# First layer's experts: the loads of the modulation columns issued by GpSimd's queue instead of SyncE's

## The chip, the cores and the metric

The kernel runs on one core of a Trainium2 chip. The metric is the device time of one execution in microseconds (us), as the median of several runs. Engines are named as the profile names them: PE is TensorE (matmuls; PEld is its weight loads, which overlap the matmuls), DVE is VectorE, ACT is ScalarE, POOL is GpSimd, SP is SyncE. A DMA is issued by an engine's instruction queue and then moved by the core's 16 DMA engines. In the profile's table of DMA queues, q1 (hardware) carries what SP issues and q0 (software) what POOL issues.

## The reference, cut to what matters

The reference is a two-layer transformer over 1024 latent tokens and 256 context tokens of width 1024. In each layer a conditioning vector is turned into six modulation vectors, attention and a convolution mix the tokens, and a mixture of 16 experts follows, in which every expert picks its 128 best latent tokens (and, in the first layer alone, its 32 best context tokens):

```python
def adaln(cond, w_mod_l, b_mod_l, n_chunks):
    m = jax.nn.silu(cond) @ w_mod_l[:, :n_chunks * D_MODEL] + b_mod_l[:n_chunks * D_MODEL]
    return jnp.split(m, n_chunks, axis=-1)

def ec_moe(h, w_router, w_gate, w_up, w_down):
    ...
    g, idx = lax.top_k(jnp.swapaxes(aff, 1, 2), cap)
    xs = jax.vmap(lambda hb, ib: hb[ib])(h, idx)
    hid = jax.nn.silu(jnp.einsum('becd,edf->becf', xs, w_gate)) * jnp.einsum('becd,edf->becf', xs, w_up)
    ye = jnp.einsum('becf,efd->becd', hid, w_down) * g[..., None].astype(h.dtype)
    return jax.vmap(lambda yb, ib: jnp.zeros((n_tok, d), h.dtype).at[ib.reshape(-1)].add(yb.reshape(-1, d)))(ye, idx)
```

The modulation of the second layer (`adaln` with that layer's weights) depends on nothing but the conditioning vector. The kernel computes most of it while the first layer's experts run, and the change touches the loads for that.

## The kernel before, in words

**The experts of the first layer.** The loop in `moe` takes 192 steps, numbered i: 16 experts e, each with 12 chunks c of weights of 1 MB (c 0 to 7 are gate and up, c 8 to 11 are down). A chunk lands in a buffer called `raw`, `more` or `srow` (a ring of nine buffers), ACT rounds it to `hi` (line 2078), DVE takes the remainder to `lo` (line 2084), and PE multiplies with both: 12 matmuls per step for the latent tokens (lines 2158 and 2262; of every three, the second is the one with `lo`, and the first of a step's twelve is one with `hi`) and 16 narrow ones for the context tokens straight from the raw chunk (lines 2169 and 2250). In step i, DVE prepares the `lo` of chunk i + 2, and SP issues the load of chunk i + 9, which waits until PE has read the chunk that stands in the same buffer (`w_load`, line 2073).

**POOL** has only DMAs to issue in this stage, four per expert, all with row indices: at c = 2 it gathers the next expert's tokens (`xg` and `xgc`, lines 2111 and 2116), and at the end of c = 11 it adds the expert's result to the sums in DRAM (`s_accc` and `s_acc`, lines 2284 and 2296), after DVE has made `yoc` and `yo`.

**The modulation columns.** In steps with i % 7 == 1 the next of 24 tiles `adw` of 1 MB is loaded (`adaln_load`, line 359), until the list `ad` is empty (i = 1, 8, 15, ... 162). There is one buffer for it. In later steps with i % 7 in 4, 5, 6 or 0 (not where c is 7 or 8), DVE multiplies a half of the tile with the conditioning row and sums it up (`adaln_col`, line 365, written `adj<-adw`): two such instructions in a step, two or four for a tile. Since 7 and 12 have no common divisor, the load falls on every c in turn.

**What sets the order.** The stage runs under `manual_schedule`: each engine and each queue takes its instructions in the order in which this loop writes them, and waits at each until what it needs is there. So DVE's `lo` of a later chunk stands behind the `adj` of the step before.

Of the kernel before, what the change touches and what calls it, by code (L numbers as in the profile page):

```python
# [208 lines left out]
class Kern:  # L209
# [145 lines left out]
        cm.__exit__(None, None, None)  # L355
        self.close(2)

    def adaln_load(self, w, l, t):
        self.nc.sync.dma_start(w, self.d["wmt"][(l * 48 + t - 12) // 2])

    def adaln_col(self, w, junk, l, t, i):

# [1724 lines left out]
    def moe(self, l, out):  # L2087
        nc, d = self.nc, self.d
# [20 lines left out]
        def gather(e):  # L2109
            x = p.tile([128, D], F32, name="xg", bufs=1)  # L2110
            nc.gpsimd.indirect_dma_start(out=x, out_offset=None, in_=self.s_h2,
                                         in_offset=bass.IndirectOffsetOnAxis(ap=idx[:, e:e + 1], axis=0))
            xc = None
            if not last:
                xc = p.tile([32, D], F32, name="xgc", bufs=1)
                nc.gpsimd.indirect_dma_start(out=xc, out_offset=None, in_=self.s_h2c,
                                             in_offset=bass.IndirectOffsetOnAxis(ap=idxc[:32, e:e + 1], axis=0))
            S["x", e] = (x, xc)
# [31 lines left out]
        def mm_gu0(e, c, ns=(0, 2, 1, 3)):  # L2150
            hi, lo = S["w", e, c]
            xt = S["xt", e]
            if c == 0:
                S["gu", e] = [rot(ps, [128, 512], F32, "gu", nb) for _ in range(4)]
            o = S["gu", e]
            for n in ns:
                for i, (a, w) in enumerate(three(hi, lo)):
                    nc.tensor.matmul(o[n], xt[:, c, a], w[:, n], start=c == 0 and i == 0, stop=c == 7 and i == 2)  # L2158
# [20 lines left out]
        def ev_gu0(e, n):  # L2179
            o = S["gu", e]  # L2180
            s = S["s", e, n] = p.tile([128, 512], F32, name="sg", bufs=2)
            nc.scalar.activation(s, o[n], AF.Silu)
            nc.vector.tensor_tensor(s, s, o[2 + n], op=ALU.mult)
# [22 lines left out]
        def mm_gu1(e, c):  # L2206
            hi, lo = S.pop(("w", e, c))
            xt = S["xt", e]
            n, r = divmod(c, 4)
            u, kh = divmod(r, 2)  # L2210
            if kh == 0:
                S["gu", e, n, u] = rot(ps, [128, 512], F32, "gu", 8)
            o = S["gu", e, n, u]
            for k in range(4):
                kk = kh * 4 + k
                nc.tensor.matmul(o, xt[:, kk, 0], hi[:, k], start=kk == 0, stop=False)  # L2216
                nc.tensor.matmul(o, xt[:, kk, 1], hi[:, k], start=False, stop=False)  # L2217
                nc.tensor.matmul(o, xt[:, kk, 0], lo[:, k], start=False, stop=kk == 7)  # L2218

        def ev_gu1(e, c, st):  # L2220
            n, r = divmod(c, 4)
            if st == 0 and r == 1:
                s = p.tile([128, 512], F32, name="sg", bufs=2)
                nc.scalar.activation(s, S.pop(("gu", e, n, 0)), AF.Silu)
                S["s", e, n] = s
            elif st == 0 and r == 3:
                s = S["s", e, n]
                nc.vector.tensor_tensor(s, s, S.pop(("gu", e, n, 1)), op=ALU.mult)
            elif st == 1 and r == 3:
                s = S.pop(("s", e, n))  # L2230
                if n == 0:
                    S["hid", e] = rot(p, [128, KC, 2, 128], F32R, "hid", 1)
                hd = S["hid", e]
                t = rot(ps, [128, 4, 128], F32, "gu", 8)
                for j in range(4):
                    nc.tensor.transpose(t[:, j], s[:, j * 128:(j + 1) * 128], self.ident)  # L2236
                ks = slice(n * 4, n * 4 + 4)
                nc.scalar.activation(hd[:, ks, 0], t, AF.Copy)  # L2238
                nc.vector.tensor_tensor(hd[:, ks, 1], t, hd[:, ks, 0].bitcast(F32), op=ALU.subtract)  # L2239
# [25 lines left out]
        def mm_d1(e, c):  # L2265
            hi, lo = S["w", e, c]
            hd = S["hid", e]
            n, kh = divmod(c - 8, 2)
            if kh == 0:
                S["y", e, n] = rot(ps, [128, 512], F32, "gu", 8)  # L2270
            y = S["y", e, n]
            for k in range(4):
                kk = kh * 4 + k
                nc.tensor.matmul(y, hd[:, kk, 0], hi[:, k], start=kk == 0, stop=False)  # L2274
                nc.tensor.matmul(y, hd[:, kk, 1], hi[:, k], start=False, stop=False)  # L2275
                nc.tensor.matmul(y, hd[:, kk, 0], lo[:, k], start=False, stop=kk == 7)  # L2276
# [11 lines left out]
        def ev_d(e, n):  # L2288
            ns = slice(n * 512, n * 512 + 512)
            y = S["y", e, n]  # L2290
            if n == 0:
                S["yo", e] = rot(p, [128, D], F32, "yo", 1)
            yo = S["yo", e]
            nc.vector.scalar_tensor_tensor(yo[:, ns], y, g[:, e:e + 1], self.g2[0][:, ns], op0=ALU.mult, op1=ALU.mult)  # L2294
            if n == 1:
                nc.gpsimd.indirect_dma_start(out=self.s_acc[l],  # L2296
                                             out_offset=bass.IndirectOffsetOnAxis(ap=idx[:, e:e + 1], axis=0),
                                             in_=yo, in_offset=None, compute_op=ALU.add)
# [30 lines left out]
        ad, todo = [], []  # L2329
        if not last:  # L2330

            ad = [t for j in range(8) for t in (2 * j, 16 + 4 * j, 18 + 4 * j)]
# [8 lines left out]
        for i in range(n - 2 if last else n - 4):  # L2341
            e, c = steps[i] if i < n else (None, None)
            pe, pc = steps[i - 1] if i > 0 else (None, None)
            if c == 2 and e + 1 < NE:
                gather(e + 1)

            def weights():
                if m <= i + m - 1 < n:
                    self.w_hi(i + m - 1)
                if m <= i + m - 2 < n:  # L2350
                    self.w_lo(l, i + m - 2, nc.vector)
            if last:
                if c < 8:
                    mm_gu1(e, c)
                else:
                    mm_d1(e, c)
                if pc is not None and pc < 8:
                    ev_gu1(pe, pc, 0)
                elif pc is not None and pc % 2:
                    ev_d(pe, pc // 2 - 4)  # L2360
                weights()
            elif c < 8:

                if c % 2 == 0:
                    mm_gu0(e, c)
                    mm_gc(e, c)
                else:
                    mm_gc(e, c)
                    if c == 7:
                        ev_gc(e)  # L2370
                    mm_gu0(e, c)
                if c < 7:
                    weights()
                else:
                    ev_gu0(e, 0)
                    ev_gu0(e, 1)
                    hprep(e, 0)
                    if e + 1 < NE:
                        xprep_c(e + 1)
                    hprep_c(e)  # L2380
                    weights()
                    if e + 1 < NE:
                        xprep(e + 1)
            else:
                if c % 2 == 0:
                    mm_d0(e, c)
                    if c == 8:
                        hprep(e, 1)
                    mm_dc(e, c)
                else:  # L2390
                    mm_dc(e, c)
                    mm_d0(e, c)
                weights()
                if c == 11:
                    ev_dc(e)
                    for h in range(2):
                        ev_d(e, h)
            while nl < n and nl - len(self.ring) <= (i + m - 2 if last else i):
                self.w_load(l, nl)
                nl += 1  # L2400
            if last and pc is not None and pc < 8:
                ev_gu1(pe, pc, 1)
            if last and i > n - 12:
                spare(i - n + 11)
            if ad and i % 7 == 1:
                adw = p.tile([128, 2, D], F32, name="adw")
                self.adaln_load(adw, l + 1, ad[0])
                todo = self.adaln_items(l + 1, ad.pop(0))
            elif todo and i % 7 in (4, 5, 6, 0) and c not in (7, 8):
                for f in todo[:2]:  # L2410
                    f(adw, p.tile([128, D], BF16, name="adj"))
                todo = todo[2:]
            if last and c == 9 and e + 1 < NE:
                xprep(e + 1)
# [166 lines left out]
```

## Time and profile before

| | |
|---|---|
| Median of 3 runs | 2855.28 us (2850.66 to 2855.35) |
| Profiled execution | 2855.14 us, of which the profile's span is 2853.4 us |
| Busy in the span: PE, DVE, ACT, POOL | 91%, 73%, 55%, 31% |
| First layer's experts, in the span | about 780 to 1570 us |
| Loads of `adw` in that stage | 24 of 1 MB, issued by SP |

The page gives busy times over the whole span; what the change is worth is read from the stretch of the first layer's experts. "Idle before" in a row is the time in which the engine did nothing ahead of that instruction, with the one that ended the wait behind the arrow. Times at a row's start count from the start of the span.

### The profile page before, as it was taken

Reading aid. Unit: us, or ns where it says so; the run is one execution under the profiler, and the core shown is the slowest. Engines: PE = TensorE matmul, PEld = TensorE weight load, DVE = VectorE, ACT = ScalarE, POOL = GpSimd, SP = SyncE. Lnnn points to the kernel's source line nnn. Section 1 sums busy time; section 2 is a strip of 40 time slices with the busy share of each in tenths; the row PEclk is TensorE's granted clock in tenths of the full one; section 3 lists DMA queues with packets and bytes.
Section 4 is the critical chain, followed back from the end, with each engine's and each line's share of the span. In section 5 each row is a group of like instructions: output and inputs, shape, how many; then the busy total and the mean of one; then the engine's idle time right before and its main releaser. Section 6 shows DMA issues by size and latency. Waiting matters only on the chain. (4 is left out here: it accounts for less than half of the span.)

```text
span 2853.4 us, 34425 instructions
## 1 busy us (share of the span) xinstructions
PE 2585.3 (91%) x12313; PEld 1861.0 (65%) x12313; DVE 2085.5 (73%) x2803; ACT 1559.2 (55%) x1920; POOL 883.7 (31%) x649
## 2 busy tenths in 40 slices
PE   7998999979499999999999599999993899999995
PEld 4986555568466666666666588655573677777774
DVE  6366467768777878787876925566588788888888
ACT  3224678622456555565655434686322577777774
POOL 3046677432410213121130308684132011111113
PEclk8999999989699999999999799999996899999997
DMA  6254644593588988889885415663456699999983
GB/s 252 67 177 156 189 147 124 151 261 119 195 308 304 321 328 307 333 309 343 306 316 196 149 60 181 174 176 93 143 195 250 237 368 373 371 372 374 374 331 139
DMA packets 204342, 682.69 MB, mean 239 GB/s; under 512 B 25637, under 2 KB 97630, under 8 KB 148870
## 3 DMA queue, kind: packets, MB, share of 16 engines
q1 hardware_dynamic: 191834, 641.23, 61.8%
q0 software_dynamic: 12336, 39.25, 5.7%
q8 instruction: 97, 1.59, 0.2%
q14 instruction: 75, 0.61, 0.1%
HBM read 600.45 MB, written 79.84 MB: 238 GB/s over the span
## 5 line engine op out<-in xcount | busy, mean ns | idle before, releaser
L2078 ACT ACTIVATE hi<-raw 128x2048 fp32r<-128x2048 f32 x264 | 505.1, 1916 | 172.0 <-PE gu L2158 78.8
L2084 DVE TENSOR_TENSOR lo<-raw,hi 128x2048 fp32r<-128x2048 f32 x259 | 582.9, 2283 | 13.6 <-ACT hi L2078 13.5
L1258 POOL TENSOR_TENSOR cy<-cy,csq 128x512 f32<-128x512 f32 (+1 forms) x300 | 372.7, 1256 | 111.0 <-ACT csq L1254 102.2
L2158 PE MATMUL gu<-hi,xt 128*128 128x512 f32 x1024 | 343.7, 404 | 0.0
L1184 PE MATMUL O<-P,v 128*65 128x512 f32 (+7 forms) x592 | 275.4, 555 | 7.9 <-ACT P L1177 7.7
L2078 ACT ACTIVATE hi<-more 128x2048 fp32r<-128x2048 f32 x105 | 200.5, 1915 | 139.6 <-PE gu L2158 112.5
L2296 POOL DMA_INDIRECT s_acc<-yo,i x31 | 122.2, 3942 | 492.8 <-DVE yo L2294 488.2
L2084 DVE TENSOR_TENSOR lo<-more,hi 128x2048 fp32r<-128x2048 f32 x105 | 237.2, 2285 | 32.8 <-ACT hi L2078 32.6
L2158 PEld LDWEIGHTS gu<-hi,xt 128*128 128x128 f32 x1024 | 193.5, 189 | 97.8 <-issue 53.6
L1254 ACT ACTIVATE csq<-ch,cw 128x512 f32<-128x512 f32 (+1 forms) x300 | 198.1, 673 | 39.0 <-POOL cy L1258 33.2
L2284 POOL DMA_INDIRECT s_accc<-yoc,i x16 | 23.6, 1474 | 621.6 <-DVE yoc L2283 621.6
L2216 PE MATMUL gu<-hi,xt 128*128 128x512 f32 x512 | 204.1, 399 | 0.0
L2158 PE MATMUL gu<-lo,xt 128*128 128x512 f32 x512 | 203.5, 398 | 0.0
L2217 PE MATMUL gu<-hi,xt 128*128 128x512 f32 x512 | 202.6, 396 | 0.0
L2218 PE MATMUL gu<-lo,xt 128*128 128x512 f32 x512 | 202.3, 395 | 0.0
L735 PE MATMUL pj<-hhi,whi 128*128 128x512 f32 (+1 forms) x512 | 188.4, 368 | 8.8 <-ACT whi L248 8.8
L737 PE MATMUL pj<-hhi,wlo 128*128 128x512 f32 (+1 forms) x512 | 188.0, 367 | 1.1 <-DVE wlo L251 1.0
L736 PE MATMUL pj<-hlo,whi 128*128 128x512 f32 (+1 forms) x512 | 187.6, 366 | 0.0
L2262 PE MATMUL gu<-hi,hid 128*128 128x512 f32 x512 | 173.0, 404 | 0.0
L365 DVE CUSTOM_DVE_ANT_0 adj<-adw,srow,bmod 128x1024 bf16<-128x1024 f32 x96 | 132.9, 1384 | 50.0 <-DMA adw<-in_wmt 48.4
L1177 ACT ACTIVATE P<-ST 128x512 f32<-128x512 f32 (+1 forms) x200 | 114.6, 581 | 55.1 <-PE ST L1160 30.1
L1736 PE MATMUL po<-hi,ohi 128*128 128x512 f32 x288 | 121.9, 423 | 19.3 <-DVE ohi L1714 18.2
(320 smaller groups left out, 5736.1 us busy)
## 6 DMA issues: line engine op xcount, KB each, us to landing
raw<-in_wmoe SPq DMA_DIRECT2D x264, 1024.0 KB
more<-in_wmoe SPq DMA_DIRECT2D x105, 1024.0 KB
adw<-in_wmt SPq DMA_DIRECT2D x24, 1024.0 KB
srow<-in_wmoe SPq DMA_DIRECT2D x15, 1024.0 KB
wraw<-in_win SPq DMA_DIRECT2D x26, 512.0 KB
x<-in_x SPq DMA_DIRECT2D x16, 512.0 KB
adw<-in_wmt SPq DMA_DIRECT2D x16, 512.0 KB
q<-s_q SPq DMA_DIRECT2D x64, 128.0 KB
```

Source lines behind the costliest of these rows:

```text
L735: nc.tensor.matmul(o[:, :w], whi[:, k], hhi[:, k, sl], start=k == 0, stop=False)
L736: nc.tensor.matmul(o[:, :w], whi[:, k], hlo[:, k, sl], start=False, stop=False)
L737: nc.tensor.matmul(o[:, :w], wlo[:, k], hhi[:, k, sl], start=False, stop=k == 7)
L1184: nc.tensor.matmul(o[:V1, o0:o0 + w], self.v[:, t["kt"], t["v"] * V1:t["v"] * V1 + V1], t["P"][:, :w], start=t["first"], stop=t["last"] is ...
L1254: nc.scalar.activation(z[:, :w], h, AF.Copy, scale=c)
L1258: nc.gpsimd.tensor_tensor(st["y"], st["y"], st.pop(("z", t))[:, :w], op=ALU.add)
L2078: self.nc.scalar.activation(h, self.S["raw", i], AF.Copy)
L2084: eng.tensor_tensor(lo, r, h.bitcast(F32), op=ALU.subtract)
L2158: nc.tensor.matmul(o[n], xt[:, c, a], w[:, n], start=c == 0 and i == 0, stop=c == 7 and i == 2)
L2216: nc.tensor.matmul(o, xt[:, kk, 0], hi[:, k], start=kk == 0, stop=False)
L2217: nc.tensor.matmul(o, xt[:, kk, 1], hi[:, k], start=False, stop=False)
L2218: nc.tensor.matmul(o, xt[:, kk, 0], lo[:, k], start=False, stop=kk == 7)
```

## The change

`adaln_load` takes the queue as an argument, and the one call in the experts' loop passes POOL's. The loads in the first layer's start (`adaln_first`) and in the attention stay on SP's queue, as do all loads of expert weights.

```diff
-    def adaln_load(self, w, l, t):
-        self.nc.sync.dma_start(w, self.d["wmt"][(l * 48 + t - 12) // 2])
+    def adaln_load(self, w, l, t, eng=None):
+        (eng or self.nc.sync).dma_start(w, self.d["wmt"][(l * 48 + t - 12) // 2])
...
             if ad and i % 7 == 1:
                 adw = p.tile([128, 2, D], F32, name="adw")
-                self.adaln_load(adw, l + 1, ad[0])
+                self.adaln_load(adw, l + 1, ad[0], nc.gpsimd)
                 todo = self.adaln_items(l + 1, ad.pop(0))
```

PE, DVE and ACT keep their instructions in the same order. On SP's queue the 24 rows go; here around the load of step 71, between the loads of weight chunks:

```order
 L2073 DMA more_8902<-in_wmoe 128x2048
 L2073 DMA more_8937<-in_wmoe 128x2048
-L359 DMA adw<-in_wmt 128x2048
 L2073 DMA raw_8966<-in_wmoe 128x2048
 L2073 DMA raw_8988<-in_wmoe 128x2048
```

The weight loads stand in the order they had, with one load of 1 MB less among them.

On POOL's queue they come in between the DMAs with row indices; here from the end of expert 2 (`s_accc` and `s_acc` with `yoc_7858` and `yo_7863`) to the end of expert 3:

```order
 L2284 DMA s_accc<-yoc_7858,i_6746 512x512
 L2296 DMA s_acc<-yo_7863,i_6721 1024x1024
-L2111 DMA xg<-s_h,i_6721 128x1024
-L2116 DMA xgc<-s_h2c,i_6743 32x1024
+L359 DMA adw<-in_wmt 128x2048
+L2111 DMA xg<-s_h,i_6721 128x1024
+L2116 DMA xgc<-s_h2c,i_6743 32x1024
+L359 DMA adw<-in_wmt 128x2048
 L2284 DMA s_accc<-yoc_8214,i_6746 512x512
 L2296 DMA s_acc<-yo_8219,i_6721 1024x1024
```

The first `adw` (step 36, c = 0) now stands right behind the two additions of expert 2 and ahead of the gathers; the second (step 43, c = 7) stands behind the gathers and ahead of the next additions.

The same at the end of expert 5 (`yo_8933`), where the load of step 71 (c = 11) and that of step 78 (c = 6) come in:

```order
 L2284 DMA s_accc<-yoc_8928,i_6746 512x512
 L2296 DMA s_acc<-yo_8933,i_6721 1024x1024
-L2111 DMA xg<-s_h,i_6721 128x1024
-L2116 DMA xgc<-s_h2c,i_6743 32x1024
+L359 DMA adw<-in_wmt 128x2048
+L2111 DMA xg<-s_h,i_6721 128x1024
+L2116 DMA xgc<-s_h2c,i_6743 32x1024
+L359 DMA adw<-in_wmt 128x2048
 L2284 DMA s_accc<-yoc_9284,i_6746 512x512
```

The load of step 71 stands behind the additions too, and takes the place in POOL's queue that the gather of `xg` had. Of the 24 loads, those of steps 36, 71, 85, 120 and 155 (c = 0, 11, 1, 0, 11) stand so, right behind the additions of an expert; those of steps 15, 50, 99 and 134 (c = 2 or 3) stand right behind the gathers; the other 15 stand where POOL has only the coming additions to wait for.

## Rows read from the trace of the kernel before

**Rows 1.** Busy time in stretches of the first layer's experts: start and end, length, busy time of PE, PEld, DVE, ACT, POOL, granted clock of PE as a share of full speed, share of the DMA engines, GB/s.
```profile
800.00:1080.00 280.00, 279.37 (x1536) 181.78 (x1534) 224.73 (x185) 166.63 (x137) 42.91 (x20) 1.00 0.85 316
1080.00:1430.00 350.00, 346.32 (x1904) 224.76 (x1905) 284.67 (x233) 201.41 (x162) 74.62 (x30) 1.00 0.87 320
```
**Rows 2.** Waits from 780 to 1490 us, of POOL, DVE and PE: who waited for whom, us in total, times, the longest.
```profile
POOL s_accc L2284 <- DVE yoc L2283: 552.0, 14, 49.7
...
DVE adj L365 <- DMA adw<-in_wmt: 14.5, 7, 4.5
...
PE gu L2169 <- DVE yo L2294: 4.3, 2, 2.3
```
**Rows 3.** PE's timeline at the first of its two waits for DVE's `yo`: start, length, instruction.
```profile
1081.38 1.92 PE L2169 MATMUL gu<-raw,xct 128*32 128x512 f32 x16 [2.02 <-DVE yo L2294]
```
**Rows 4.** Two loads of `adw` on SP's queue (steps 36 and 71): start and length of the issue.
```profile
934.32 0.47 SPq L359 DMA_DIRECT2D adw<-in_wmt  x1
...
1077.12 0.33 SPq L359 DMA_DIRECT2D adw<-in_wmt  x1
```
**Rows 5.** POOL's timeline: the addition of expert 2 and the gather of `xg` behind it; the addition of expert 3 and the gather of `xgc` behind it; the addition of expert 5 and the gather behind it; then the gathers behind the additions of experts 6, 9 and 12; the length is the time in which POOL writes the DMA's descriptors.
```profile
933.72 7.32 POOL L2296 DMA_INDIRECT s_acc<-yo,i  x1 [0.30 <-issue]
941.34 1.56 POOL L2111 DMA_INDIRECT xg<-s_h,i  x1 [0.30 <-issue]
...
982.52 1.92 POOL L2296 DMA_INDIRECT s_acc<-yo,i  x1 [0.30 <-issue]
...
987.69 1.78 POOL L2116 DMA_INDIRECT xgc<-s_h2c,i  x1 [0.30 <-issue]
...
1082.73 8.52 POOL L2296 DMA_INDIRECT s_acc<-yo,i  x1 [0.30 <-issue]
1091.55 2.65 POOL L2111 DMA_INDIRECT xg<-s_h,i  x1 [0.30 <-issue]
...
1138.70 1.54 POOL L2111 DMA_INDIRECT xg<-s_h,i  x1 [0.30 <-issue]
...
1285.15 1.55 POOL L2111 DMA_INDIRECT xg<-s_h,i  x1 [0.30 <-issue]
...
1435.62 2.65 POOL L2111 DMA_INDIRECT xg<-s_h,i  x1 [0.30 <-issue]
```
**Rows 6.** The DMAs of POOL's queue in narrow windows: the last number is us from the start of the issue to landing. First the single gather of `xg` at 780.15, which no addition precedes; then `s_acc` and `xg` of 930 to 946; `xg` of 1080 to 1098; `xgc` of 985 to 989; `xg` of 1129 to 1144, 1275 to 1290 and 1425 to 1440.
```profile
xg<-s_h,i POOLq DMA_INDIRECT x1, 4.5
...
s_acc<-yo,i POOLq DMA_INDIRECT x1, 17.2
xg<-s_h,i POOLq DMA_INDIRECT x1, 14.3
...
xg<-s_h,i POOLq DMA_INDIRECT x1, 13.5
...
xgc<-s_h2c,i POOLq DMA_INDIRECT x1, 13.0
...
xg<-s_h,i POOLq DMA_INDIRECT x1, 13.2
...
xg<-s_h,i POOLq DMA_INDIRECT x1, 14.9
...
xg<-s_h,i POOLq DMA_INDIRECT x1, 11.7
```
**Rows 7.** The direct loads that POOL issues in the kernel before (in the attention): the group in POOL's lines from 300 to 460 us (busy time, mean ns of one), and one of them in the table of DMA issues with KB and us to landing.
```profile
L1241 POOL DMA_DIRECT2D ch<-s_cv x4 | 2.3, 577 | 0.1
...
ch<-s_cv POOLq DMA_DIRECT2D x1, 263.5 KB, 4.2
```
**Rows 8.** DVE's timeline at the use of `adw` of steps 36 and 71: start, length, instruction, idle time before it.
```profile
943.06 1.28 DVE L365 CUSTOM_DVE_ANT_0 adj<-adw,srow,bmod 128x1024 bf16<-128x1024 f32 x1 [1.03 <-DMA adw<-in_wmt]
...
945.60 4.49 DVE L2084 TENSOR_TENSOR lo<-more,hi 128x2048 fp32r<-128x2048 f32 x2
...
1088.52 1.27 DVE L365 CUSTOM_DVE_ANT_0 adj<-adw,srow,bmod 128x1024 bf16<-128x1024 f32 x1
```
**Rows 9.** PE's weight loads: the first matmul that needs the `lo` which DVE makes right behind the `adj` of steps 36, 50, 71, 85, 120 and 155.
```profile
952.89 0.19 PEld L2158 LDWEIGHTS gu<-lo,xt 128*128 128x128 f32 x1
...
1011.86 0.19 PEld L2262 LDWEIGHTS gu<-lo,hid 128*128 128x128 f32 x1
...
1098.64 0.19 PEld L2158 LDWEIGHTS gu<-lo,xt 128*128 128x128 f32 x1
...
1155.10 0.19 PEld L2158 LDWEIGHTS gu<-lo,xt 128*128 128x128 f32 x1
...
1296.69 0.19 PEld L2158 LDWEIGHTS gu<-lo,xt 128*128 128x128 f32 x1
...
1442.71 0.19 PEld L2158 LDWEIGHTS gu<-lo,xt 128*128 128x128 f32 x1
```
**Rows 10.** Stretches around an idle time of PE in the second layer (2036 to 2041), columns as in rows 1; the last row is the stretch from the end of the wait of rows 3 on.
```profile
2036.00:2041.00 5.00, 0.29 (x1) 0.00 (x1) 1.33 (x3) 4.67 (x4) 1.75 (x3) 0.83 0.81 247
2041.00:2046.00 5.00, 4.97 (x12) 3.94 (x13) 4.96 (x6) 1.32 (x1) 0.00 (x0) 0.50 1.11 309
2046.00:2050.00 4.00, 4.00 (x19) 3.26 (x18) 4.00 (x4) 0.00 (x0) 0.00 (x0) 0.98 1.02 388
...
1081.00:1090.00 9.00, 8.62 (x52) 5.23 (x56) 8.96 (x8) 3.06 (x3) 8.70 (x2) 1.00 0.85 290
```

## The prediction

> **What bounds the kernel now.** The first view is busy time by stretches of the first layer's experts: PE works through 279.4 of 280 us at full clock, then 346.3 of 350, while DVE is at 80% and the DMA engines at 85 to 87% [rows 1]. So the stage lasts as long as PE's matmuls, and a load is worth time only where it makes PE wait. The second view is who waited for whom. DVE waits seven times for `adw`, 14.5 us in all; POOL waits 552 us for `yoc`, so it mostly stands at the addition of the running expert; PE's one real wait is 4.3 us, twice, for DVE's `yo` [rows 2]. At that place PE stands 2.0 us [rows 3]. That wait comes from DVE's order and not from a late tile. So there are at most 4.3 us to win here, and the question is what a later `adw` costs.
>
> **The change part by part.** *SP's queue* loses 24 issues of 0.3 to 0.5 us [rows 4] and 24 MB. The weights' loads behind them start a little earlier, but of the waits in that view PE's is for `yo` alone and none is for a weight load, so I take nothing.
>
> *POOL's queue* gains 24 issues. The direct loads that POOL issues elsewhere take 577 ns each [rows 7], so 24 x 0.6 = 14 us of an engine that waits 552 us: nothing by itself. What counts is where they stand. Fifteen stand where POOL waits only for the next addition; these start as soon as DVE has done with the tile before, some steps earlier than on SP, and cost nothing. Four stand behind the gathers, five right behind an expert's additions.
>
> *The five behind the additions.* Two delays meet. POOL issues in order: the load of step 71 left SP at 1077.1 [rows 4], but POOL writes the descriptors of `s_acc` from 1082.73 for 8.52 us and can take the next DMA at 1091.55, where the gather of `xg` stands now [rows 5]. And the transfers of POOL's queue land one after the other: `s_acc` of expert 2 lands at 933.72 + 17.2 = 950.9, the gather of 0.5 MB behind it at 941.34 + 14.3 = 955.6, so 4.7 us later, although a gather with nothing ahead of it lands 4.5 us after its issue [rows 5, 6]. The moved load takes this gather's place exactly. How long its 1 MB then takes is not in the trace. By bytes from the gather it is 9.4 us, by the 388 GB/s of another stretch [rows 10] 2.7 us. I take the gather's own 4.7 us, the nearest row (same place, also 128 rows). So I say that `adw` lands when `xg` landed: 955.6, 1105.1, 1151.9, 1300.1 and 1447.3 for steps 36, 71, 85, 120 and 155 [rows 5, 6].
>
> What that costs: DVE needs 4.8 us from the start of `adj` to the end of the next `lo` (943.06 to the middle of the pair from 945.60 that lasts 4.49) [rows 8]. PE needs that `lo` at 952.89, 1098.64, 1155.10, 1296.69 and 1442.71 [rows 9]. The latest harmless landing is 4.8 us before each: 948.1, 1093.8, 1150.3, 1291.9, 1437.9. The differences are 7.5, 11.3, 1.6, 8.2 and 9.4 us: PE stands 38 us in all. Before, DVE reached these tiles at 943 and 1088.5 [rows 8]. Behind `lo` on DVE's queue stand the following `lo`, one per step of PE and 2.3 us each against a step of some 4 us, so DVE catches up within two or three steps and nothing more is lost; the gathers, now behind the load, land about 5 us later, but their users are on PE behind the same stall.
>
> *The four behind the gathers.* For step 50, `xgc` lands at 987.69 + 13.0 = 1000.7 [rows 5, 6], `adw` 4.7 us later at 1005.4, and harmless is until 1011.86 - 4.8 = 1007.1 [rows 9]. Cover of 1.7 us: I take nothing. If the transfer took 9.4 us, it and its twin of step 134 would lose 3 us each.
>
> *PE's clock.* After standing from 2036.3 to 2041, PE worked 5 us at a granted clock of 0.50, its lower level of 1.2 GHz, before it was back at 2.4 GHz; after the 2.0 us of rows 3 the clock stays 1.00 [rows 3, 10]. So a long stop costs another 2.5 us: four stops of 7.5 us and more, 10 us; the short one none. Its bounds are 0 and, with the steps 50 and 134 stopping too, 15.
>
> Sum against the profiled execution: 2855.1 + 38 + 10 = 2903 us; that execution is 0.1 us from the median of the runs, so the number stands for the median too. Ends: with 2.7 us for the transfer, 2 us less at four places and 1.6 at the fifth, some 2.5 us less at steps 71 and 155 where POOL writes faster once DVE stands, and no clock loss, 38 - 9.6 - 5 = 23, so 2878; with 9.4 us, 38 + 5 x 4.7 + 6 + 15 = 83, so 2938.
>
> On descriptors the Trainium skill (SBUF - State Buffer, "SBUF: two separate sides") warns that a DMA issued from POOL can starve while DVE holds the port that both share, and that one issued from SP can't. The row beside it: the same addition takes 1.92 us to write at 982.52 and 8.52 at 1082.73 [rows 5], which fits, though the direct loads show 577 ns [rows 7]. By the rule the moved loads could be stretched too, which is the high rival below; by the direct row they are not.
>
> **The rivals.** *No queueing behind the additions.* If the loads share the DMA engines with `s_acc` instead of following it, they land as SP's did, 943.06 - 934.32 = 8.7 us after the issue [rows 4, 8], so at 950.0, 1100.3, 1147.4, 1293.9 and 1444.3: 1.9 + 6.5 + 0 + 2.0 + 6.4 = 17 us late, with two long stops 5 us of clock, 2877 us. With the 4.5 us of a lone gather only the steps 71 and 155 are late, by 2 us each: 2860. For it: the DMA engines are not full. Against it: the gather behind each addition lands 12 to 15 us after its issue [rows 6]. A page has the rule: the Trainium skill (DMA: Bandwidth & Descriptors, "Issuing engines are not separate DMA queues") says that DMAs of all queues interleave on the same 16 engines and that the issuer saves only issue time. By that alone it would come out near no change; it holds between queues, while here the delay arises within POOL's.
>
> *Not slower.* The earlier loads end DVE's 14.5 us of waiting, DVE runs ahead, and PE's two waits of 4.3 us [rows 2] go: 2851. This decides only if the late five land within 6.8, 2.3, 11.6, 6.7 and 2.3 us of POOL's issue (harmless time less the issue in rows 5). The fastest rows are 4.5 and 4.2 us [rows 6, 7], too slow for the second and the fifth, and PE waited for `yo` there, not behind an `adw`.
>
> *Slower still.* POOL's writing of the load is stretched as that of `s_acc` is, or the transfer goes by bytes: the high end, 2938 us. Against it: while DVE stands waiting, it leaves the port to POOL.
>
> **How the numbers follow.** My forecast, queueing with 38 us of stops and 10 of clock, has 0.68, with a range of its own from 2880 to 2925. The first rival has 0.15 (2860 to 2877), the second 0.05, the third 0.12. The range for 8 in 10 is 2867 to 2930: it takes in most of the first rival and the lower half of the third. A measurement of this kernel can tell 0.2%, 5.7 us, from no change: faster by more has 0.02, within it 0.06 (the second rival and the fastest of the first), slower 0.92.
>
> **What would show it.** In the changed kernel's waits, DVE must wait for `adw` five times for more than 8 us, right after the additions of experts 2, 5, 6, 9 and 12, and hardly elsewhere; PE must wait for DVE's `lo`, where it did not, about 38 us in four or five stops; the granted clock must show 0.50 for some us behind each long one; `xg` must land some 5 us later behind the same additions. The stages after the experts must keep their length. The step on the landing is wrong if `adw` lands well before `s_acc` plus 4.7 us; the step on the cover is wrong if DVE waits and PE does not. The prediction fails if the span of the experts' stage grows by under 12 us or over 75.

## The result and the profile after

The changed kernel takes 2893.25 us (median of 4 runs, 2887.9 to 2895.06) against 2855.31 us before in the same comparison: a ratio of 1.0127, with a 95% interval of 1.0109 to 1.0145. It is slower by 38 us. The profiled execution is the fastest of the four: it took 2887.9 us with a span of 2886.1 us, 32.8 us more than the 2853.4 us of before.

Where the time went is read from one instruction that runs once per expert, ACT's `sc`. The view of its line gives the shortest, median and longest duration in ns, then the start of the first and of the last one. In the kernel before:

```profile
L2174 ACT ACTIVATE sc<-gu x16: 592/592/593, 811.3 to 1548.0; 64x512 f32<-64x512 f32 x16
```

In the changed kernel:

```profile
L2174 ACT ACTIVATE sc<-gu x16: 591/592/593, 811.6 to 1584.1; 64x512 f32<-64x512 f32 x16
```

From first to last that is 736.7 us before and 772.5 us after, 35.8 us more. Everything outside it is 3 us shorter (35.8 - 32.8). So in this execution the whole loss lies in the first layer's experts; what the other three lost besides, 5 to 7 us, has no profile. This distance is called "the stage" below.

Who waited for whom in the changed kernel, from 780 to 1520 us (columns as in [rows 2]):

```profile
POOL s_accc L2284 <- DVE yoc L2283: 428.2, 14, 44.4
POOL adw L359 <- DVE modc L365: 146.1, 11, 23.1
DVE adj L365 <- DMA adw<-in_wmt: 62.1, 7, 11.7
...
PE gu L2158 <- DVE lo L2084: 15.9, 4, 6.2
...
PE gu L2192 <- DVE sg L2183: 6.1, 3, 2.8
PE gu L2169 <- DVE yo L2294: 4.3, 2, 2.3
```

DVE waits 62.1 us for `adw` where it waited 14.5 [rows 2]. There are seven waits in both, so they became longer: 8.9 us each on the mean, from 2.1. Two new lines stand for PE: 15.9 us for `lo` and 6.1 us for `sg`, 22.0 us together. The old wait for `yo` is unchanged. POOL's new waits for `modc` (the buffer of `adw` is still in use) take 146 us and cost nothing: they come out of the time in which it stood waiting for `yoc`.

The chain at one place, behind the addition of expert 5 (step 71). POOL's timeline, columns as in [rows 5]:

```profile
1089.68 1.49 POOL L2284 DMA_INDIRECT s_accc<-yoc,i  x1 [44.12 <-DVE yoc L2283]
1091.47 7.30 POOL L2296 DMA_INDIRECT s_acc<-yo,i  x1 [0.30 <-issue]
1098.19 1.20 POOL L359 DMA_DIRECT2D adw<-in_wmt  x1
1099.69 1.01 POOL L2111 DMA_INDIRECT xg<-s_h,i  x1 [0.30 <-issue]
```

The landing of what was issued there, from 1089 to 1101 us (columns as in [rows 6]):

```profile
adw<-in_wmt POOLq DMA_DIRECT2D x1, 1024.0 KB, 10.8
s_accc<-yoc,i POOLq DMA_INDIRECT x1, 4.4
s_acc<-yo,i POOLq DMA_INDIRECT x1, 12.0
xg<-s_h,i POOLq DMA_INDIRECT x1, 13.1
```

So `s_acc` lands at 1091.47 + 12.0 = 1103.5, `adw` at 1109.0 and `xg` at 1112.8: one after the other, although their descriptors were written within 9.2 us. What POOL's queue (q0) moved shows the same order. From 1099 to 1103, from 1103 to 1108 and from 1108 to 1114 us (packets, MB, share of the 16 DMA engines):

```profile
q0 software_dynamic: 143, 0.52, 85.7%
...
q0 software_dynamic: 128, 1.04, 49.1%
...
q0 software_dynamic: 208, 0.66, 28.4%
```

0.52 MB is the size of `s_acc`, 1.04 MB that of `adw`, and 0.66 MB that of the two gathers. At the five places the load lands 9.2 to 11.3 us after its issue. Six loads ahead of which POOL's queue had nothing left to move took 6.3 to 9.5 us; this is the one issued at 1173.14:

```profile
adw<-in_wmt POOLq DMA_DIRECT2D x1, 1024.0 KB, 9.5
```

What DVE and PE do with it, DVE first (columns as in [rows 8]), steps 36 and 71:

```profile
952.00 1.28 DVE L365 CUSTOM_DVE_ANT_0 adj<-adw,srow,bmod 128x1024 bf16<-128x1024 f32 x1 [9.75 <-DMA adw<-in_wmt]
...
1109.06 1.28 DVE L365 CUSTOM_DVE_ANT_0 adj<-adw,srow,bmod 128x1024 bf16<-128x1024 f32 x1 [11.74 <-DMA adw<-in_wmt]
```

PE's timeline at the same two steps:

```profile
956.89 0.80 PE L2158 MATMUL gu<-lo,xt 128*128 128x512 f32 x1 [3.38 <-DVE lo L2084]
...
1113.94 0.80 PE L2158 MATMUL gu<-lo,xt 128*128 128x512 f32 x1 [6.18 <-DVE lo L2084]
```

DVE stands 11.74 us, PE 6.18: the difference is what DVE had in hand. In each of the two rows the matmul starts 4.9 us after the start of `adj`, which is the path of `adj`, `adj`, `lo` from [rows 8].

Behind each such stop PE runs at half clock. Stretches of the changed kernel, columns as in [rows 1]:

```profile
953.20:956.80 3.60, 0.31 (x2) 0.00 (x0) 3.56 (x6) 1.91 (x1) 0.57 (x1) 0.97 1.03 337
956.80:960.00 3.20, 3.11 (x7) 2.48 (x8) 3.20 (x3) 0.00 (x0) 0.00 (x0) 0.50 1.00 412
960.00:964.00 4.00, 4.00 (x26) 1.89 (x25) 1.23 (x1) 0.95 (x2) 0.00 (x0) 1.00 0.80 291
...
1018.10:1021.40 3.30, 3.30 (x13) 3.01 (x13) 3.12 (x3) 3.24 (x5) 0.00 (x0) 0.50 0.78 328
...
800.00:1584.00 784.00, 757.75 (x4086) 490.37 (x4084) 593.52 (x476) 434.93 (x349) 147.10 (x81) 0.98 0.81 296
```

The first three rows show the stop of step 36, then 3.2 us at 0.50 (1.2 GHz) in which 7 matmuls were done, then full clock. The fourth stands behind a stop of only 1.65 us. Over the whole stage the mean clock is 0.98, where the rows of before show 1.00 [rows 1]. The sum: 22.0 us of new waits leave 35.8 - 22.0 = 13.8 us to the clock, and 2% of 784 us is 16 us with a rounded 2%. Some 1.6 us of this stand behind no new wait: the clock is at 0.50 from 1455.0 to 1458.3 too, behind the second of the old waits for `yo`.

### The profile page after: what moved, and what is told of

The parts are those of the page before. It is cut to its first block, busy times and chain, and to the rows that moved or that the text cites. A ratio compares the mean times of both kernels' runs of the same rounds, so it can differ in the third digit from the quotient of the medians.

```text
span 2886.1 us, 34447 instructions
## 1 busy us (share of the span) xinstructions
PE 2597.1 (90%) x12313; PEld 1867.1 (65%) x12313; DVE 2083.9 (72%) x2803; ACT 1559.1 (54%) x1920; POOL 887.0 (31%) x673
## 5 line engine op out<-in xcount | busy, mean ns | idle before, releaser
L2084 DVE TENSOR_TENSOR lo<-raw,hi 128x2048 fp32r<-128x2048 f32 x259 | 582.6, 2283 | 13.1 <-ACT hi L2078 13.1
L2158 PE MATMUL gu<-lo,xt 128*128 128x512 f32 x512 | 206.3, 403 | 15.9 <-DVE lo L2084 15.9
L1177 ACT ACTIVATE P<-ST 128x512 f32<-128x512 f32 (+1 forms) x200 | 114.4, 580 | 50.2 <-PE ST L1160 24.1
```

The source lines that it names most:

```text
L2084: eng.tensor_tensor(lo, r, h.bitcast(F32), op=ALU.subtract)
```

## The experiments

The theory under test ("place"): only the loads that stand right behind an expert's additions cost time, because on POOL's queue they follow `s_acc`. Its first rival ("queue"): 24 loads on POOL's queue cost time wherever they stand. Each edit is against the changed kernel unless it is said otherwise; each ratio is against runs of the kernel before on the same chip.

### Which loads cost: a, b, c

a_five_on_sp gives the five loads behind additions back to SP, and with them that of step 1 (c = 1), so that 18 stay on POOL's queue:

```diff
-                self.adaln_load(adw, l + 1, ad[0], nc.gpsimd)
+                self.adaln_load(adw, l + 1, ad[0], nc.sync if c in (11, 0, 1) else nc.gpsimd)
```

> The loads of steps 36, 71, 85, 120 and 155 (and that of step 1) go back to SP's queue, the other 18 stay on POOL's. Place theory (a load costs only where it stands behind an expert's additions or gathers): in the changed kernel's trace these five cost 5.2 + 7.8 + 3.4 + 5.1 + 6.2 = 28 of the stage's 36 us, the steps 50 and 134 another 8; so about 8 us over before, 2863 us. Queue theory (each load costs the same because POOL writes its descriptors or disturbs DVE): 18/24 of 36, so 27 us over before, 2882 us.

Measured: 2859.91 us, ratio 1.0021 (1.0005 to 1.0038), stage 739.5 us. DVE waits 14.5 us for `adw`; of the new waits of PE one for `sg` is left, 2.2 us.

b_seven_on_sp also gives back two of the loads behind the gathers (`c in (11, 0, 1, 2)`: steps 50 and 134); 16 stay on POOL's queue.

> As the run before, with the loads of steps 50 and 134 on SP's queue too; 16 loads stay on POOL's. Place theory: nothing is late, 2855 us within 4 us, PE waits as in the kernel before. Queue theory: 16/24 of 36, 24 us over before, 2879 us.

Measured: 2855.65 us, ratio 1.0 (0.9989 to 1.0011), stage 736.8 us, as before. Its waits from 780 to 1520 us:

```profile
DVE adj L365 <- DMA adw<-in_wmt: 11.1, 5, 3.6
...
PE gu L2169 <- DVE yo L2294: 4.3, 2, 2.3
```

c_five_on_pool is the complement: only the five on POOL's queue.

```diff
+                self.adaln_load(adw, l + 1, ad[0], nc.gpsimd if c in (11, 0, 1) and i > 1 else nc.sync)
```

> Only the loads of steps 36, 71, 85, 120 and 155 are on POOL's queue, 19 stay on SP's. Place theory: 28 us over before, 2883 us. Queue theory: 5/24 of 36, 7 us over before, 2862 us.

Measured: 2886.39 us, ratio 1.0111 (1.0094 to 1.0127), stage 762.6 us, 25.9 more than before. Its waits:

```profile
DVE adj L365 <- DMA adw<-in_wmt: 56.6, 9, 12.4
...
PE gu L2158 <- DVE lo L2084: 16.1, 4, 6.8
```

Five loads alone bring 26 of the 36 us of the stage. Eighteen of the others alone bring 2.8 (a), which go with steps 50 and 134 (b); the last 16 bring nothing. The two parts add up to 28.7 us and not to 35.8, mostly because steps 50 and 134 cost less in a than in the changed kernel: PE stops at step 50 alone, 2.2 us, with the clock at 1.00 behind it (1014.3 to 1017.7 us), and the load of step 134 landed 22.8 us after its `s_accc` had started, where it landed after 25.5 in the changed kernel and stopped PE. That the loads beside them matter to this is not shown. "Queue" is refuted: b has 16 loads on POOL and the time of before.

### Whether POOL's queue costs anything by itself: d, j

d_early_on_pool keeps all 24 on POOL, but issues the five ahead of the additions, at the expert's last step:

```diff
                 if c == 11:
+                    for j in range(i, i + 3):
+                        if ad and j % 7 == 1:
+                            adw = p.tile([128, 2, D], F32, name="adw")
+                            self.adaln_load(adw, l + 1, ad[0], nc.gpsimd)
+                            early = j
                     ev_dc(e)
...
             if ad and i % 7 == 1:
-                adw = p.tile([128, 2, D], F32, name="adw")
-                self.adaln_load(adw, l + 1, ad[0], nc.gpsimd)
+                if i != early:
+                    adw = p.tile([128, 2, D], F32, name="adw")
+                    self.adaln_load(adw, l + 1, ad[0], nc.gpsimd)
```

> All 24 loads on POOL's queue, but the five are written ahead of the additions of the expert that ends instead of behind them. Place theory: the five land in time, the steps 50 and 134 stay late, 8 us over before, 2863 us. Queue theory: no change against the changed kernel, 2892 us. If the additions, now behind a load of 1 MB in the same queue, held somebody up, it would be PE or DVE waiting for s_acc's buffer yo, and the time would stay above 2870.

Measured: 2864.52 us, ratio 1.0026 (1.0012 to 1.0041), stage 747.5 us. The waits:

```profile
DVE adj L365 <- DMA adw<-in_wmt: 14.2, 2, 7.5
...
PE gu L2192 <- DVE sg L2183: 4.3, 2, 2.5
```

The waits for `lo` are gone. Two for `sg` are left, which are steps 50 and 134, still behind the gathers. j_all_early moves these two as well (the same lines ahead of `gather(e + 1)` at c = 2):

> As the run with the five ahead of the additions, and the loads of steps 50 and 134 (c = 2) now also ahead of the gathers: all 24 on POOL's queue, none behind a DMA it could follow. Place theory: nobody waits long for adw, the stage is as long as before (736.7 us from the first to the last silu of the context rows), 2855 us within 5 us. If traffic on POOL's queue had a cost besides, the stage would stay 3 us or more longer.

Measured: 2855.92 us, ratio 1.0002 (0.9993 to 1.0012), stage 740.0 us. The waits:

```profile
PE gu L2169 <- DVE yo L2294: 4.3, 2, 2.3
DVE adj L365 <- DMA adw<-in_wmt: 3.4, 2, 2.1
```

All 24 loads are on POOL's queue, and the time is that of before; against d the stage is 7.5 us shorter, which steps 50 and 134 cost there. Against before the stage is 3.3 us longer, by the expectation the sign of a cost of the traffic on POOL's queue. The clock shows where they went, in two stretches behind the two old waits for `yo` (columns as in [rows 1]):

```profile
1079.20:1082.50 3.30, 3.30 (x13) 1.74 (x6) 3.30 (x2) 0.00 (x0) 3.17 (x1) 0.50 0.90 236
...
1424.00:1427.20 3.20, 3.20 (x17) 0.64 (x10) 3.20 (x3) 0.00 (x0) 2.90 (x2) 0.50 0.53 77
```

3.3 and 3.2 us at half clock lose 1.65 + 1.6 = 3.3 us, where the same wait of 2.02 us left the clock at 1.00 before [rows 3, 10]. Whether POOL's queue has a part in that is open: behind these two waits the clock fell at least once in the changed kernel and in c, d, f, g, j and k, and never in before, a, b and i; but in h, with all 24 loads on POOL's queue too, it stays at 1.00 behind both (1081.2 to 1084.6 and 1426.1 to 1429.5 us). Beyond these 3.3 us the engine that issues does not matter here; the place in the queue does. The Trainium skill (DMA: Bandwidth & Descriptors, "Issuing engines are not separate DMA queues") says that DMAs started by any engine run on the same 16 DMA engines and interleave; b and j, alike in time within 0.1%, agree.

### Which of the two delays: f, g

f_between puts the five between `s_accc` and `s_acc` (the loop of d, one line lower, behind `ev_dc(e)`).

> All 24 loads on POOL's queue; the five stand between s_accc and s_acc of the expert that ends, so they still wait for DVE's yoc but no longer for the descriptors and the transfer of s_acc. If s_acc is what makes them late: the load of step 71 is issued some 1.8 us after s_accc starts, lands 6 to 9 us later (about 3 us before the latest harmless time) and the five cost nothing; only steps 50 and 134 stay, 2863 us. If the wait for yoc is what matters: about 2890 us, as in the changed kernel.

Measured: 2864.86 us, ratio 1.0028 (1.0015 to 1.0041), stage 746.7 us; DVE waits 19.7 us for `adw`, PE 3.2 us for `sg` and never for `lo`. At step 71 the load lands 10.4 us after the start of `s_accc` (1078.28 + 9.4 against 1077.31) and not 19.4, within what DVE and PE can do without. The time is that of d: `s_accc` ahead costs none that shows, so of the two additions it is `s_acc` that makes the load too late.

g_narrow_addition leaves the loads where the change put them and adds only 16 of the 1024 columns in the first layer:

```diff
+                w = D if last else 16
-                nc.gpsimd.indirect_dma_start(out=self.s_acc[l],
+                nc.gpsimd.indirect_dma_start(out=self.s_acc[l].rearrange("a (b c) -> (a b) c", c=w),
...
-                                             in_=yo, in_offset=None, compute_op=ALU.add)
+                                             in_=yo[:, :w], in_offset=None, compute_op=ALU.add)
```

> The changed kernel, with the first layer's latent additions cut from 1024 columns to 16 (the rest of the sums is left out): POOL still writes the descriptors of 128 rows, but the transfer moves 8 KB instead of 512 KB. If both delays count as in the forecast, the five land about 4 us earlier each and lose some 3 us each with their clock, 50 and 134 come in time: 2867 to 2875 us. If only POOL's writing counts: 2893 us. If only the transfer queue counts: 2855 us.

Measured: 2866.35 us, ratio 1.0028 (1.0011 to 1.0044), but its profiled execution took 2858.17 us, with a stage of 739.9 us. POOL's timeline at step 71:

```profile
1080.50 7.30 POOL L2297 DMA_INDIRECT s_acc<-yo,i  x1 [0.30 <-issue]
1087.21 1.20 POOL L359 DMA_DIRECT2D adw<-in_wmt  x1
```

Its landings from 1080 to 1089 us:

```profile
adw<-in_wmt POOLq DMA_DIRECT2D x1, 1024.0 KB, 5.8
s_acc<-yo,i POOLq DMA_INDIRECT x1, 8.9
```

The descriptors take 7.30 us to write as they did, so the load leaves POOL just as late; but it now lands 5.8 us after its issue and not 10.8. DVE waits 28.5 us in all, 6.7 at most, and PE's only wait is the old one for `yo`. So in this execution POOL's order alone makes the load late by less than DVE and PE can do without; only with the transfer of `s_acc` ahead of it in the queue does PE stop. Not all that the load gained is the queue's: while it moved, SP's queue moved 0.07 MB in g (1089.1 to 1092.8 us) and 1.09 MB in the changed kernel (1103.5 to 1108.5). The profiled execution comes near the third of the expected times, the median lies just below the first. Four of the ten runs took 2855.4 to 2858.4 us, the profiled one among them, and six 2866.0 to 2869.1; what PE did in the six has no profile and stays open.

### Taking the lateness away: h, i

h_two_buffers keeps all loads in their places on POOL, but gives `adw` two buffers and loads seven steps ahead. For the space the ring of weight chunks is shortened (`MORE0 = 4` in place of 5). i_eight_buffers is the control: the kernel before with that shorter ring.

```diff
-    MORE0 = 5
+    MORE0 = 4
...
+                if i == 1:
+                    ahead = p.tile([128, 2, D], F32, name="adw0")
+                    self.adaln_load(ahead, l + 1, ad[0], nc.gpsimd)
+                adw = ahead
                 todo = self.adaln_items(l + 1, ad.pop(0))
+                if ad:
+                    ahead = p.tile([128, 2, D], F32, name=f"adw{len(ad) % 2}")
+                    self.adaln_load(ahead, l + 1, ad[0], nc.gpsimd)
```

> All 24 loads on POOL's queue and at the same places in it, but adw has two buffers and each load fetches the tile that is needed seven steps (some 27 us) later than now; room for it is made by a ring of eight weight buffers instead of nine. Lateness theory: the loads land as late as in the changed kernel and nobody waits: same time as the control with eight buffers, within 4 us. If POOL's issuing or its queue's traffic itself cost anything: above the control by up to 30 us.

> Control for the run with two buffers: the kernel before with a ring of eight weight buffers. DMA engines are busy 85 to 87% of the stage, so a ring one shorter may cost nothing (2855 us) or a few us; both theories agree.

Measured: h 2862.94 us, ratio 1.0020 (1.0010 to 1.0029), stage 738.4 us, with no wait of DVE for `adw`; i 2859.63 us, ratio 1.0017 (1.0007 to 1.0028), stage 736.8 us. The two ratios lie within each other's intervals. The loads stand behind the additions and follow them as in the changed kernel, and it costs nothing once nobody needs them soon. The small loss that both share came with the shorter ring and lies behind the stage (from its end to the end of the span 1312.7 us in h and 1311.0 in i, against 1305.4 before); why is not known.

### Why `s_acc` landed earlier: k

In the changed kernel `s_acc` landed sooner after the start of its `s_accc` than before: by 14 us and not 19 (next section). The theory: before, SP's queue had the load of `adw` to move as well in these microseconds. In the 13 us from the start of `s_accc` it moved 3.2 to 3.6 MB at the five places before, and 2.1 to 2.5 MB in the changed kernel. k_dummy_on_sp adds to the changed kernel, at each of the 24 places, a copy of 1 MB on SP's queue, from device memory to device memory, that nobody reads:

```diff
                 self.adaln_load(adw, l + 1, ad[0], nc.gpsimd)
+                nc.sync.dma_start(self.s_dummy[(i - 1) // 7], d["wmt"][i // 7])
```

> The changed kernel, and at each of the 24 places on SP's queue where the load stood a copy of 1 MB from DRAM to a spare place in DRAM that nobody reads. In the changed kernel s_acc lands 13.8 to 14.9 us after s_accc starts (18.4 to 20.0 before). If that is because SP's queue no longer moves adw at that moment, s_acc lands 18 us or more after s_accc again, adw some 5 us behind it, and the stops grow to what was forecast: 2900 to 2910 us. If it is because PE and DVE stand and the weights' loads stop with them, nothing changes: 2893 us.

Measured: 2909.36 us, ratio 1.018 (1.0155 to 1.0204), stage 786.4 us, 13.9 more than the changed kernel. The waits (line numbers are higher by one):

```profile
DVE adj L366 <- DMA adw<-in_wmt: 73.9, 7, 13.3
...
PE gu L2159 <- DVE lo L2085: 24.1, 5, 7.1
```

The dummy has no buffer to wait for, so it leaves earlier or later against the addition from place to place. SP's queue at steps 36 and 71:

```profile
935.37 0.49 SPq L2409 DMA_DIRECT2D s_dummy<-in_wmt  x1
...
1090.17 0.50 SPq L2409 DMA_DIRECT2D s_dummy<-in_wmt  x1
```

The landings from 932 to 942 us (step 36) and, behind the mark, from 1096 to 1106 us (step 71):

```profile
adw<-in_wmt POOLq DMA_DIRECT2D x1, 1024.0 KB, 14.0
...
s_acc<-yo,i POOLq DMA_INDIRECT x1, 15.8
...
adw<-in_wmt POOLq DMA_DIRECT2D x1, 1024.0 KB, 8.9
...
s_acc<-yo,i POOLq DMA_INDIRECT x1, 12.0
```

Where the dummy left just after the additions had begun (steps 36, 85 and 120) SP's queue moved 3.5 to 3.6 MB in those 13 us, and `s_acc` landed 17.6 to 18.4 us after the start of `s_accc`; where it left 7 us ahead of it (1090.17 against 1097.1 at step 71, and so at 155) it moved 2.1 to 2.2 MB, and `s_acc` landed after 13.8 us, as in the changed kernel. So one transfer of 1 MB on SP's queue at that moment costs `s_acc` some 4 us. That PE and DVE stand, the other theory of the expectation, does not make it early: they stand in k as well. In a, where the five loads are back on SP, it lands 17.9 to 19.6 us after again. For steps 71 and 155 a is the only test, and there POOL also wrote `s_acc` in 7.3 us in the changed kernel and in 8.5 before and in a. k does not tell whether this is the 1 MB's share of the DMA engines or something in how the queues take turns.

## Why the prediction was right, and where its sizes were off

The side, the mechanism and the five places held; the forecast of 2903 us was 10 us above the median, and 15 above the profiled execution, on which the working below rests. That it came so near is in part luck: its errors have opposite signs. Point by point:

**What bounds the stage.** Held. The stage grew by what PE lost: 22.0 us of new waits and the rest at half clock.

**SP's queue, and 24 issues on POOL, cost nothing.** Held as far as the runs can tell: j has every load on POOL and the time of before within its interval. But SP's emptier queue, for which the prediction took nothing, moved the landing of `s_acc`, as the size below shows. A moved load takes 717 ns to write on the mean (POOL's lines, 780 to 1520 us), and 1.2 us at the five places, while `s_acc` takes 4585 ns:

```profile
L2296 POOL DMA_INDIRECT s_acc<-yo,i x14 | 64.2, 4585 | 4.3 <-issue 4.3
...
L359 POOL DMA_DIRECT2D adw<-in_wmt x23 | 16.5, 717 | 156.4 <-DVE modc L365 146.1 <-DVE modc L369 10.3
```

That is against the high rival, in which writing the moved loads is stretched as that of `s_acc` is.

**The five behind the additions: the mechanism.** Held. c and a show that these five carry the larger part of the loss, f and the profile of g that `s_acc` ahead in the queue is what makes the load late enough. `adw` landed 4.9, 5.6, 5.8, 5.0 and 3.7 us behind `s_acc`; the prediction took 4.7.

**The five: the size.** This is the step that failed: "the moved load takes this gather's place exactly", so that `adw` lands "when `xg` landed: 955.6, 1105.1, 1151.9, 1300.1 and 1447.3". It took the landing of `s_acc` ahead as unchanged. Counted from the start of the expert's `s_accc` (starts from POOL's timeline, landings from the DMA tables, as at step 71 above), in us:

| step | `s_acc` lands, before | after | `adw` lands, forecast | measured | PE stops, forecast | measured |
|---|---|---|---|---|---|---|
| 36 | 19.0 | 14.9 | 23.7 | 19.8 | 7.5 | 3.4 |
| 71 | 20.0 | 13.8 | 24.1 | 19.4 | 11.3 | 6.2 |
| 85 | 18.4 | 13.8 | 22.6 | 19.6 | 1.6 | 1.7 |
| 120 | 18.6 | 14.6 | 24.3 | 19.6 | 8.2 | 3.3 |
| 155 | 19.8 | 14.0 | 22.3 | 17.7 | 9.4 | 3.0 |

`s_acc` lands 4 to 6 us earlier, because SP's queue has 1 MB less to move beside it: k shows this for steps 36, 85 and 120, for 71 and 155 only a speaks for it. `adw` lands 3 to 5 us earlier, and PE's stops shrink from 38 to 17.5 us. The other link of the step, how long PE can do without, held at step 36, where `adw` landed 952.0 - 948.1 = 3.9 us after the latest harmless time and PE stood 3.4. At step 85 the match of 1.6 and 1.7 us is luck: `adw` landed 3 us earlier than forecast, before the latest harmless time for `lo`, and PE stood for another tile (next point).

**The four behind the gathers.** "Cover of 1.7 us: I take nothing" was wrong for steps 50 and 134. `adw` landed 24.4 us after `s_accc` at step 50, forecast 24.7, so the landing was right. The cover was not, since it was reckoned only to the next `lo`. DVE's timeline at step 50:

```profile
1010.42 1.28 DVE L365 CUSTOM_DVE_ANT_0 adj<-adw,srow,bmod 128x1024 bf16<-128x1024 f32 x1 [6.60 <-DMA adw<-in_wmt]
...
1012.96 2.29 DVE L2084 TENSOR_TENSOR lo<-raw,hi 128x2048 fp32r<-128x2048 f32 x1
1015.17 0.68 DVE L2176 TENSOR_TENSOR sc<-sc,uc 64x512 f32<-64x512 f32 x1
1015.77 1.27 DVE L2183 TENSOR_TENSOR sg<-sg,gu 128x512 f32<-128x512 f32 x2
```

Behind `adj` and `lo` stand `sc` and `sg`, and PE's transposes wait for `sg`:

```profile
1016.50 0.66 PE L2192 MATMUL gu<-ident,sg 128*128 128x128 f32 x4 [1.65 <-DVE sg L2183]
```

Step 134 stops PE 2.8 us in the same way, and at step 85 too the wait is for `sg` and not, as forecast, for `lo`. Where the load of step 50 stands behind the gathers on POOL's queue, PE's stop is what its landing has beyond some 22.7 us from the start of `s_accc`: landing after 23.6 us it stood 0.8 us (f), 24.4 and 1.65 (the changed kernel), 24.9 and 2.2 (a), 25.2 and 2.5 (d), 26.6 and 3.8 (k). Step 50 alone is most of the difference between a and b; steps 50 and 134 with their clock are that between d and j.

**The clock.** "Four long stops, 10 us; the short one none": the row of before on which "none" rested [rows 3, 10] did not carry over. All seven new stops, down to 1.65 us, are followed by 3 us or more at 0.50; with the old wait at 1455 us the clock took some 14 us.

**The sum.** With the measured terms it is 22.0 + 13.8 = 35.8 us in the stage, against 38 + 10 = 48. Five stops were forecast 20 us too long; two stops of 4.4 us together and 4 us of clock were not forecast at all.

**The rivals.** "No queueing behind the additions" is refuted by what POOL's queue moved, one DMA after the other, and in the profile of g by the landing 5.7 to 7.1 us after the issue where it was 9.2 to 11.3. Its 17 us of late time come near the measured 17.5 only as a sum: by place it had 1.9, 6.5, 0, 2.0 and 6.4 us. "Not slower": DVE's waits became long, and PE's old waits did not go. "Slower still" fell with the 1.2 us of writing above, and `adw` landed 3.7 to 5.8 us behind `s_acc`, not 9.4.

**What should have shown.** DVE was to wait five times for more than 8 us: it did so at steps 36, 71, 120 and 155 (9.5 to 11.7 us), and 6.7 us at step 85; but steps 50 and 134 (6.6 and 7.7 us) were not among "hardly elsewhere". `xg` was to land some 5 us later: at step 71 it landed 23.1 us after `s_accc` (1099.69 + 13.1 against 1089.68), before 24.1. What the load ahead cost it, the earlier `s_acc` gave back. From the end of the stage to the end of the span it took 1302.0 us, before 1305.4. The sign set for the step on the landing, `adw` well before `s_acc` plus 4.7 us, did not show although that step failed, since it counts from an `s_acc` that itself came early.

## What to carry to other kernels

When a DMA is moved to another engine's queue, read its place in the new queue: what that engine still has to issue, and which transfer it then follows. Whether it is POOL or SP matters little beside that, and issuing it one step earlier, ahead of the engine's next blocking wait, can give back the whole loss, as in j. Reckon the new landing with the old copy of the DMA taken out, since the neighbours that shared the DMA engines with it move too; and follow the late tile through everything queued behind its first user, not only to the next tile that the critical engine reads.

## What was not expected of the hardware

- DMAs of POOL's one queue moved and landed one after the other: 1 MB issued behind `s_acc` landed 9.2 to 11.3 us after its issue, with nothing of that queue ahead 6.3 to 9.5 us after it, and behind an `s_acc` of 16 columns 5.7 to 7.1 us.
- One transfer of 1 MB on SP's queue at the moment of the addition moves the landing of `s_acc` by some 4 us (17.6 to 18.4 us from the start of `s_accc` in k, 13.8 to 14.9 in the changed kernel at the same steps).
- Short stops of PE can cost nearly as much again in clock: behind 1.65 us of standing, 3.3 us at 0.50. But the same wait of 2.02 us for `yo` was followed by a clock of 1.00 in the kernel before and by 0.50 in j. Length alone does not decide: in c a stop of 3.54 us that ended at 1309.69 was followed by 1.00 (columns as in [rows 1]). What decides was not found.

```profile
1309.70:1313.10 3.40, 3.40 (x19) 2.27 (x23) 3.40 (x2) 0.00 (x0) 0.00 (x0) 1.00 0.93 386
```
